# Rotation tables: one pass for all blocks, copies within DRAM, and plain loads of a block's tables

## The chip, the cores and the metric

The kernel runs on one core of one Trainium2 chip. The metric is the device time of one execution in microseconds. The core has five instruction queues that run side by side: TensorE (PE, matmuls), VectorE (DVE), ScalarE (ACT), GpSimd (POOL) and SyncE (SP), which in this kernel issues every transfer. Each of them works strictly in the order in which its instructions stand.

## What is computed

Two layers of a streaming encoder over 2048 frames of width 1024. Each layer projects its input, runs four groups of attention heads, gates them, projects their concatenation and normalises. Two of the groups rotate queries and keys by the frame's position; the change is about the tables of that rotation.

```python
def _rope(x, positions):
    d = x.shape[-1]
    inv_freq = ROPE_THETA ** (-jnp.arange(0, d, 2, dtype=jnp.float32) / d)
    ang = positions.astype(jnp.float32)[..., None] * inv_freq
    cos = jnp.cos(ang)[:, :, None, :]
    sin = jnp.sin(ang)[:, :, None, :]
    x1, x2 = jnp.split(x.astype(jnp.float32), 2, axis=-1)
    out = jnp.concatenate([x1 * cos - x2 * sin, x2 * cos + x1 * sin], axis=-1)
...
def _layer(x, mem, positions, w_in, ...):
    proj = x @ w_in
    ...
    ya = _banded_chunk_attention(aq, ak, av, A_PREV_CHUNKS, rel_bias=rel_bias)
    yb = _mla(bcq, bckv, bkr, positions, mla_q_norm, w_uq, mla_kv_norm, w_ukv)   # rotates 32 columns
    qc = _rope(cq, positions); kc = _rope(ck, positions)                         # 64 columns
    yc = _banded_chunk_attention(qc, kc, cv, SWA_PREV_CHUNKS, sinks=swa_sinks)
    ym = _memory_attention(mq, mem, w_mem_kv)
    gated = jnp.concatenate([ya * silu(ag), yb * silu(bg), yc * silu(cg), ym * silu(mg)], axis=-1)
    return _layer_norm(alpha * x + gated @ w_out, ln_gain, ln_bias)
```

## The kernel before

The frames are cut into four blocks of 512 (`BT`). A layer's first phase walks over the blocks; for each there are six units: `unit_c` (sliding window), `unit_m` (memory tokens) and `unit_a` (chunked attention), each for two pairs of heads, 0 and 1. A unit has a list of steps (`fill`: projections and what is made of them) and a list of score banks. `drive` runs the banks in order and mixes the next unit's steps among them. Then come `unit_b` (latent attention) over the blocks, and a third phase with the output projection and the norm. All products are done in two parts, a rounded high part and the rest (`whi`, `wlo`, `xh`, `xl`, `ph`, `pl`), whose splits are ACT's, DVE's and POOL's main work. What is written there is not yet the order on the engines: a scheduler in the compiler sorts the instructions of the whole program again, engine by engine, and each engine then keeps to that order.

A table has 128 rows (partitions) and 512 columns (frames). Its rows repeat: group 0 (`unit_c`, 64 columns to rotate) has 32 frequencies, four times over, group 1 (latents and `unit_b`) 16, eight times over. The sine's rows carry a sign that alternates by halves, from columns 2 and 3 of the constants `rc`. `trig(b, gs)` makes the cosine and sine of block `b` for the groups `gs`: it loads the positions to all rows, multiplies by the frequency, reduces the angle to the sine's range by a chain of DVE operations, takes two sines on ACT, and stores both tables to DRAM. It is called for block 0 and group 0 at the start, in `mem_kv`, among loads of the memory tokens (`xt<-in_mem`) and of x (`xt<-in_xT`); for block 0 and group 1 at the head of the first `unit_m`; and for block b + 1, both groups, as one step of `unit_a(l, b, 1)`. Where tables are used, two loads fetch them into the two tiles `cts`: `cts[0]` the cosine, `cts[1]` the sine. This is done 40 times in the program, in both layers. The rope of `unit_c` multiplies by both, moves the rows of the sine's product by four transfers (`us<-u`) and adds.

Steps draw temporary tiles from a ring called `tmp`, which `pi`, `ang`, `kk`, `xt` and many others share: a tile takes a buffer that earlier ones have left. PE waits for the splits and for the transfers of row maxima (`Y<-mr`) and copies (`Y<-Y`).

Of the kernel before, what the change touches and what calls it, by code (L numbers as in the profile page):

```python
# [11 lines left out]
F32 = mybir.dt.float32  # L12
# [4 lines left out]
OP = mybir.AluOpType  # L17
# [132 lines left out]
def hybrid(ctx, tc, x, mem, positions, w_in, rel_bias, q_norm, w_uq, kv_norm, w_ukv,  # L150
# [55 lines left out]
    def tmp(name, dt=F32):  # L206
        return sb.tile([128, BT], dt, name=name, tag="tmp", bufs=5)

    def rowcast(src, off, n):
        return bass.AP(tensor=src.tensor, offset=src.offset + off, ap=[[0, 128], [1, n]])  # L210
# [56 lines left out]

    cosT, sinT, memkv = {}, {}, {}
    h_src = [x[0, t * 128:(t + 1) * 128, :] for t in range(S // 128)]
# [8 lines left out]

    def trig(b, gs=(0, 1)):
        pi = tmp("pi", I32)  # L280
        dma(pi, rowcast(positions, b * BT, BT))
        pf = tmp("pf")
        nc.vector.tensor_copy(pf, pi)
        for g in gs:
            ang, kk = tmp("ang"), tmp("kk")
            nc.vector.tensor_scalar(ang, pf, rc[:, g:g + 1], None, op0=OP.mult)
            nc.vector.tensor_scalar(kk, ang, float(np.float32(1.0 / TWO_PI)), ROUND, op0=OP.mult, op1=OP.add)
            nc.vector.tensor_scalar(kk, kk, -ROUND, None, op0=OP.add)
            for pc in (PC1, PC2, PC3):
                stt(ang, kk, -pc, ang, op0=OP.mult, op1=OP.add)  # L290
            nc.vector.tensor_scalar(ang, ang, 3.1415925, -3.1415925, op0=OP.min, op1=OP.max)
            nc.vector.tensor_scalar(kk, ang, -1.0, None, op0=OP.mult)
            tt(kk, kk, ang, op=OP.max)
            nc.vector.tensor_scalar(kk, kk, -1.0, float(np.float32(math.pi / 2)), op0=OP.mult, op1=OP.add)
            act(ang, ang, AF.Sin)
            act(kk, kk, AF.Sin)
            nc.vector.tensor_scalar(ang, ang, rc[:, 2 + g:3 + g], None, op0=OP.mult)
            cosT[g, b] = dram.tile([128, BT], F32, name=f"cos{g}{b}")
            sinT[g, b] = dram.tile([128, BT], F32, name=f"sin{g}{b}")
            dma(cosT[g, b], kk)  # L300
            dma(sinT[g, b], ang)

# [429 lines left out]
    def unit_c(l, b, p, D):  # L732
# [4 lines left out]
        def tabl():  # L737
            dma(cts[0], cosT[0, b])
            dma(cts[1], sinT[0, b])
            if p == 0 and b:  # L740
                for k in range(2):
                    dma(f32(Kc[k][0])[:, 0:128], f32(Kc[k][0])[:, BT:BT + 128])
                    dma(f32(Kc[k][1])[0:64, 0:128], f32(Kc[k][1])[0:64, BT:BT + 128])
                dma(f32(Vc)[:, 0], f32(Vc)[:, 4])
# [81 lines left out]
    def latent(l, b, k, p, D):  # L826
# [6 lines left out]
        if k == 0:  # L833
            dma(cts[0], cosT[1, b])
            dma(cts[1], sinT[1, b])
            D["sums", b] = sb.tile([128, 3, 4], F32, name="sums", bufs=2)
# [119 lines left out]
    def unit_b(l, b, p, D):  # L956
# [13 lines left out]
        def loads():  # L970
            for k in (0, 2):
                dma(f32(lat[k]), f32(D["lathl"][k, b]).rearrange("p (s c) -> p s c", s=2))
            for z in range(2):
                dma(f32(lat[1])[64 * z:64 * z + 64, 0], f32(D["lathl"][1, b])[:, BT * z:BT * z + BT])
            dma(cts[0], cosT[1, b])
            dma(cts[1], sinT[1, b])
            for i in range(2):
# [231 lines left out]
    def mem_kv(kq):  # L1209
# [4 lines left out]
        dma(rc, rope_c)  # L1214
        trig(0, (0,))
        wload(1)
# [217 lines left out]
    for l in range(L):  # L1434
# [13 lines left out]
        else:  # L1448
            kq()
            load_mem(l)  # L1450
        units = []
        for b in range(NB):
            us = [unit_c(l, b, 0, D), None, None, None, None, None]
# [12 lines left out]
            if l == 0 and b == 0:  # L1466
                us[1][0].insert(0, (0.0, lambda: trig(0, (1,))))
            if l == 0 and b + 1 < NB:
                us[5][0].insert(2, (0.0, lambda b=b: trig(b + 1)))
            units += us  # L1470
# [64 lines left out]
```

## Time and profile before

| | |
|---|---|
| three runs, us | 2652.08, 2657.08, 2656.91; median 2656.91 |
| the profiled execution, us | 2656.69; its span 2654.9 |
| busy share of the span | PE 95%, DVE 70%, ACT 47%, POOL 40% |
| mean granted clock of PE | 0.981 |

The span runs from the first to the last instruction of the profiled execution. Busy is the time in which an engine had an instruction in work; for PE it is modelled, since matmuls overlap. The granted clock is the share of PE's full speed that the chip allowed.

### The profile page before, as it was taken

To read this page: it belongs to the slowest core of one execution; us is meant where nothing else is said; L and a number is where in the kernel's file an instruction comes from. 1 tells how busy PE (TensorE), PEld (TensorE's weight loads), DVE (VectorE), ACT (ScalarE), POOL (GpSimd) and SP (SyncE) were. 2 spreads that over 40 slices of the span, in tenths; PEclk is the share of its full clock that TensorE was granted. 3 is DMA by queue.
4 is the path that set the end of the run, shared out by engine and by line. 5 is a ranking of instruction groups with operands and counts; after the bars stand their busy time and mean duration, and the time that the engine had idled before them with its cause. 6 is when DMAs were issued, how large, how long until landed. Compare 5 with 4: busy or idle time off the path is not lost.

```text
span 2654.9 us, 36284 instructions
## 1 busy us (share of the span) xinstructions
PE 2518.4 (95%) x12312; PEld 2079.1 (78%) x12312; DVE 1871.5 (70%) x3309; ACT 1258.6 (47%) x2251; POOL 1070.8 (40%) x835
## 2 busy tenths in 40 slices
PE   7899999999999899989999999999999999998998
PEld 6777877877888788768877778788788777876786
DVE  5667768658666876878776566567577578588786
ACT  4545455545544566660025444454544455666200
POOL 4243334343344343354343434434433433435343
PEclk9999999999999999999999999999999999999999
DMA  6555345345335523254445443443443453233432
GB/s 213 162 158 164 109 137 159 113 128 165 107 125 158 158 77 92 76 160 140 146 138 154 156 144 121 134 139 118 137 136 115 145 166 108 62 116 96 151 122 85
DMA packets 176442, 350.90 MB, mean 132 GB/s; under 512 B 25688, under 2 KB 48944, under 8 KB 176256
## 3 DMA queue, kind: packets, MB, share of 16 engines
q1 hardware_dynamic: 176256, 348.58, 41.9%
q8 instruction: 98, 1.61, 0.3%
q14 instruction: 88, 0.72, 0.1%
HBM read 247.43 MB, written 68.02 MB: 119 GB/s over the span
## 4 chain that ended last, share of the span: by engine, by line
PE 60%; DVE 12%; issue 9%; DMA 5%; POOL 5%; ACT 3%; SPq 1%; POOLq 0%; DVEq 0%; ACTq 0%
PE pp L350 29%; PE sc L350 10%; PE pv L350 10%; PE mx L350 4%; PE po L350 3%; POOL xr L182 2%; PE up L350 2%; DVE pl L174 2%; DVE mcol L186 1%; DVE Y L174 1%; PE pst L856 1%; DVE gd L190 1%; DVE xl L174 1%; DVE e L190 1%; PE pvt L445 1%
## 5 line engine op out<-in xcount | busy, mean ns | idle before, releaser
L182 POOL TENSOR_TENSOR wlo<-raw,whi 128x1024 fp32r<-128x1024 f32 (+1 forms) x192 | 460.0, 2396 | 658.9 <-ACT whi L170 602.0
L350 PE MATMUL pp<-xh,whi 128*128 128x512 f32 x1472 | 590.7, 401 | 8.8 <-DVE Y L174 6.7
L350 PE MATMUL pp<-xl,whi 128*128 128x512 f32 x1472 | 582.5, 396 | 5.1 <-DVE xl L174 5.1
L350 PE MATMUL pp<-xh,wlo 128*128 128x512 f32 x1472 | 579.6, 394 | 0.0
L350 PE MATMUL sc<-Y 96*128 96x512 f32 (+16 forms) x1840 | 462.4, 354 | 14.6 <-DMA Y<-mr 8.7
L170 ACT ACTIVATE ph<-sc 128x512 fp32r<-128x512 f32 (+1 forms) x504 | 291.9, 579 | 321.8 <-PE sc L350 313.8
L174 DVE TENSOR_TENSOR pl<-p,ph 128x512 fp32r<-128x512 f32 (+2 forms) x361 | 300.9, 835 | 166.7 <-ACT p L170 157.2
L350 PEld LDWEIGHTS sc<-Y 96*128 96x128 f32 (+6 forms) x1840 | 319.7, 195 | 60.1 <-issue 9.5
L350 PE MATMUL pv<-ph,Y 128*128 128x512 f32 (+3 forms) x1396 | 357.3, 338 | 6.6 <-DVE e L178 5.3
L170 ACT ACTIVATE whi<-raw 128x1024 fp32r<-128x1024 f32 x192 | 203.5, 1060 | 326.9 <-PE pp L350 120.1
L350 PEld LDWEIGHTS pp<-xh,whi 128*128 128x128 f32 x1472 | 279.2, 190 | 64.8 <-issue 7.8
L350 PEld LDWEIGHTS pp<-xh,wlo 128*128 128x128 f32 x1472 | 278.3, 189 | 58.9
L350 PEld LDWEIGHTS pp<-xl,whi 128*128 128x128 f32 x1472 | 279.4, 190 | 49.7 <-DVE xl L174 6.6
L170 ACT ACTIVATE p<-sc 128x512 f32<-128x512 f32 (+1 forms) x504 | 291.1, 578 | 4.4 <-DVE pl L174 3.5
L182 POOL TENSOR_TENSOR pl<-p,ph 128x512 fp32r<-128x512 f32 (+1 forms) x143 | 186.9, 1307 | 263.0 <-ACT p L170 221.6
L350 PEld LDWEIGHTS pv<-ph,Y 128*128 128x128 f32 x1396 | 248.6, 191 | 42.5 <-issue 6.4
L350 PE MATMUL mx<-Y 128*128 128x256 f32 (+6 forms) x800 | 248.5, 338 | 21.1 <-DVE Y L178 10.6
L350 PE MATMUL pv<-pl,Y 128*128 128x512 f32 (+3 forms) x698 | 239.5, 343 | 22.8 <-DVE pl L174 14.9
L495 DVE CUSTOM_DVE_ANT_0 mx<-mx,bts 128x128 f32<-128x128 f32 (+3 forms) x352 | 171.8, 495 | 74.5 <-PE mx L350 67.4
L350 PEld LDWEIGHTS mx<-Y 128*128 128x128 f32 (+1 forms) x800 | 148.7, 191 | 75.2 <-DVE Y L178 17.4
L182 POOL TENSOR_TENSOR g<-g,e 128x128 f32<-128x128 f32 x192 | 117.1, 618 | 205.9 <-DVE e L190 198.6
L350 PE MATMUL po<-Y 128*128 128x512 f32 x768 | 177.3, 390 | 1.7 <-DVE xl L174 1.7
(241 smaller groups left out, 3763.8 us busy)
## 6 DMA issues: line engine op xcount, KB each, us to landing
raw<-in_w_in_dram SPq DMA_DIRECT2D x184, 512.0 KB
Y<-Y SPq DMA_DIRECT2D x144, 128.0 KB
gr<-gT SPq DMA_DIRECT2D x64, 256.0 KB
gT<-g SPq DMA_DIRECT2D x48, 256.0 KB
cts<-sin SPq DMA_DIRECT2D x40, 256.0 KB
cts<-cos SPq DMA_DIRECT2D x40, 256.0 KB
xt<-in_xT_dram SPq DMA_DIRECT2D x32, 256.0 KB
raw<-in_w_out_dram SPq DMA_DIRECT2D x16, 512.0 KB
```

The source lines that it names most:

```text
L170: return nc.scalar.activation(out, a, fn, **kw)
L174: return nc.vector.tensor_tensor(out, a, b, **kw)
L182: return nc.gpsimd.tensor_tensor(out, a, b, **kw)
L186: return nc.vector.reduce_max(out, a, axis=AX.X)
L190: return nc.vector.reciprocal(out, a)
L350: mm(o, lhs, rhs, start=start, stop=stop)
L445: nc.tensor.transpose(pt[:, j * 128:(j + 1) * 128], vf[:, j * 128:(j + 1) * 128], ident)
L495: nc.vector.tensor_tensor_reduce(m, m, table, op0=OP.add, op1=OP.max, scale=1.0, scalar=floor, accum_out=acc)
L856: mm(ps[:, 2 * t:2 * t + 2], sf[:, 128 * t:128 * t + 128], ones_f, start=True, stop=True)
```

## The change

The positions are loaded so that rows 32b to 32b + 31 hold those of block b (`trig_pos`, four transfers of 32 rows). One pass of the chain so makes the 32 rows of all four blocks at once (for group 1, 16 frequencies, twice over). `trig(g, pi)` is the list of the chain's 13 steps; it now ends with a negated sine, made by one more DVE operation, instead of a multiplication by the signs. Cosine, sine and negated sine are stored one below the other in one DRAM tile of 384 rows. `spread(g, b)` copies block b's rows out of it into two full tables of 128 rows, from DRAM to DRAM: the repeats are in the source's access pattern. `tload` loads these two tables, where the two loads of cosine and sine stood. The pass of group 0 and the copies for block 0 are called at the start, as `trig` was. The pass of group 1 is mixed, a step at a time, among the steps of the first `unit_m`. The copies of block b + 1 are single steps of `unit_c(l, b, 1)` for group 0 and of `unit_m(l, b, 1)` for group 1.

```diff
@@ -276,29 +276,65 @@
             act(rr[0:32, 0:c1 - c0], rf[0:32, 0:c1 - c0], AF.Copy)
             dma(f32(rowt)[:, c0:c1], f32(rr)[0:32, 0:c1 - c0])
 
-    def trig(b, gs=(0, 1)):
+    def trig_pos():
+
         pi = tmp("pi", I32)
-        dma(pi, rowcast(positions, b * BT, BT))
-        pf = tmp("pf")
-        nc.vector.tensor_copy(pf, pi)
-        for g in gs:
-            ang, kk = tmp("ang"), tmp("kk")
-            nc.vector.tensor_scalar(ang, pf, rc[:, g:g + 1], None, op0=OP.mult)
-            nc.vector.tensor_scalar(kk, ang, float(np.float32(1.0 / TWO_PI)), ROUND, op0=OP.mult, op1=OP.add)
-            nc.vector.tensor_scalar(kk, kk, -ROUND, None, op0=OP.add)
-            for pc in (PC1, PC2, PC3):
-                stt(ang, kk, -pc, ang, op0=OP.mult, op1=OP.add)
-            nc.vector.tensor_scalar(ang, ang, 3.1415925, -3.1415925, op0=OP.min, op1=OP.max)
-            nc.vector.tensor_scalar(kk, ang, -1.0, None, op0=OP.mult)
-            tt(kk, kk, ang, op=OP.max)
-            nc.vector.tensor_scalar(kk, kk, -1.0, float(np.float32(math.pi / 2)), op0=OP.mult, op1=OP.add)
-            act(ang, ang, AF.Sin)
-            act(kk, kk, AF.Sin)
-            nc.vector.tensor_scalar(ang, ang, rc[:, 2 + g:3 + g], None, op0=OP.mult)
-            cosT[g, b] = dram.tile([128, BT], F32, name=f"cos{g}{b}")
-            sinT[g, b] = dram.tile([128, BT], F32, name=f"sin{g}{b}")
-            dma(cosT[g, b], kk)
-            dma(sinT[g, b], ang)
+        for b in range(NB):
+            dma(pi[32 * b:32 * b + 32], bass.AP(tensor=positions.tensor, offset=positions.offset + b * BT,
+                                                ap=[[0, 32], [1, BT]]))
+        return pi
+
+    def trig(g, pi):
+
+        st = {}
+
+        def sc(o, i, *c, **k):
+            return lambda: nc.vector.tensor_scalar(st[o], st[i], *c, **k)
+
+        def red(pc):
+            return lambda: stt(st["a"], st["k"], -pc, st["a"], op0=OP.mult, op1=OP.add)
+
+        def start():
+            st["a"], st["k"] = tmp("ang"), tmp("kk")
+            nc.vector.tensor_copy(st["k"], pi)
+
+        def sine():
+            act(st["a"], st["a"], AF.Sin)
+            act(st["k"], st["k"], AF.Sin)
+            t = trigt[g] = dram.tile([3 * 128, BT], F32, name=f"trig{g}")
+            dma(t[0:128], st["k"])
+            dma(t[128 * (1 + g):128 * (2 + g)], st["a"])
+
+        def neg():
+            st["n"] = tmp("nsin")
+            nc.vector.tensor_scalar(st["n"], st["a"], -1.0, None, op0=OP.mult)
+            dma(trigt[g][128 * (2 - g):128 * (3 - g)], st["n"])
+        return [start,
+                sc("a", "k", rc[:, g:g + 1], None, op0=OP.mult),
+                sc("k", "a", float(np.float32(1.0 / TWO_PI)), ROUND, op0=OP.mult, op1=OP.add),
+                sc("k", "k", -ROUND, None, op0=OP.add)] + [red(pc) for pc in (PC1, PC2, PC3)] + [
+                sc("a", "a", 3.1415925, -3.1415925, op0=OP.min, op1=OP.max),
+                sc("k", "a", -1.0, None, op0=OP.mult),
+                lambda: tt(st["k"], st["k"], st["a"], op=OP.max),
+                sc("k", "k", -1.0, float(np.float32(math.pi / 2)), op0=OP.mult, op1=OP.add),
+                sine, neg]
+
+    def spread(g, b):
+
+        t = trigt[g][32 * b:32 * b + 1, 0:1]
+        n = 32 >> g
+        for k, (o, ap) in enumerate(((0, [[0, 4], [BT, 32], [1, BT]]),
+                                     (128 * BT, [[0, 2 + 2 * g], [(128 + g * n) * BT, 2], [BT, n], [1, BT]]))):
+            r = tabt[g, b, k] = dram.tile([128, BT], F32, name=f"tab{g}{b}{k}")
+            i = bass.AP(tensor=t.tensor, offset=t.offset + o, ap=ap)
+            if k:
+                dma(r.rearrange("(a s n) c -> a s n c", s=2, n=n), i)
+            else:
+                dma(r.rearrange("(a n) c -> a n c", n=32), i)
+
+    def tload(g, b):
+        for k in range(2):
+            dma(cts[k], tabt[g, b, k])
@@ -735,8 +771,7 @@
         fill = []
 
         def tabl():
-            dma(cts[0], cosT[0, b])
-            dma(cts[1], sinT[0, b])
+            tload(0, b)
             if p == 0 and b:
                 for k in range(2):
                     dma(f32(Kc[k][0])[:, 0:128], f32(Kc[k][0])[:, BT:BT + 128])
@@ -831,8 +866,7 @@
         if n == 64:
             nc.gpsimd.memset(sf[64:128], 0.0)
         if k == 0:
-            dma(cts[0], cosT[1, b])
-            dma(cts[1], sinT[1, b])
+            tload(1, b)
             D["sums", b] = sb.tile([128, 3, 4], F32, name="sums", bufs=2)
         later(0.8, lambda: dma(D["lat"][k, b][:n], cf[:n]))
         if k == 1:
@@ -972,8 +1006,7 @@
                 dma(f32(lat[k]), f32(D["lathl"][k, b]).rearrange("p (s c) -> p s c", s=2))
             for z in range(2):
                 dma(f32(lat[1])[64 * z:64 * z + 64, 0], f32(D["lathl"][1, b])[:, BT * z:BT * z + BT])
-            dma(cts[0], cosT[1, b])
-            dma(cts[1], sinT[1, b])
+            tload(1, b)
             for i in range(2):
                 kh, kl = kpart(i, b)
                 dma(f32(kh)[96:101], f32(rowt)[26:31, 0:BT])
@@ -1212,7 +1245,9 @@
         wload(0)
         f()
         dma(rc, rope_c)
-        trig(0, (0,))
+        for f_ in trig(0, trig_pos()):
+            f_()
+        spread(0, 0)
         wload(1)
         run_fill(st)
         wsplit(0)
@@ -1464,9 +1500,11 @@
             if b == 0:
                 us[2] = ([(0.0, lambda: (ka(), bias_tables(l, D)))] + us[2][0], us[2][1])
             if l == 0 and b == 0:
-                us[1][0].insert(0, (0.0, lambda: trig(0, (1,))))
+                us[1] = (mix(us[1][0], [(0.0, lambda: tg.extend(trig(1, trig_pos())))]
+                             + [(0.0, lambda: tg.pop(0)())] * 13 + [(0.0, lambda: spread(1, 0))]),) + us[1][1:]
             if l == 0 and b + 1 < NB:
-                us[5][0].insert(2, (0.0, lambda b=b: trig(b + 1)))
+                for g in range(2):
+                    us[3 + g][0].insert(2, (0.0, lambda b=b, g=g: spread(g, b + 1)))
             units += us
         for p in range(2):
             for b in range(NB):
```

Three places on the engines show what this moves; buffer numbers are the program's own. The first is DVE in block 2, around its last units, where the tables of block 3 were made. Before, these twelve rows ended it (`ang` and `kk` belong to the tables; `g` and `e` are the gate's numerator and denominator, `pl` a rest, `Y` queries and keys):

```order
L174 TENSOR_TENSOR kk<-kk,ang 128x512
L291 TENSOR_SCALAR ang<-ang 128x512
L294 TENSOR_SCALAR kk<-kk 128x512
L292 TENSOR_SCALAR kk<-ang 128x512
L174 TENSOR_TENSOR Y<-pp,Y 64x512
L174 TENSOR_TENSOR kk<-kk,ang 128x512
L297 TENSOR_SCALAR ang<-ang,rc 128x512
L294 TENSOR_SCALAR kk<-kk 128x512
L297 TENSOR_SCALAR ang<-ang,rc 128x512
L174 TENSOR_TENSOR g<-pv,g 64x512
L178 SCALAR_TENSOR_TENSOR e<-e,pv 64x512
L174 TENSOR_TENSOR Y<-pp,Y 64x512
```

Now, from the rest `pl` ahead of the same gate on:

```order
L174 TENSOR_TENSOR pl<-p,ph 128x512
L174 TENSOR_TENSOR Y<-ef,Y 1x512
L190 RECIPROCAL e<-e 128x128 x2
L174 TENSOR_TENSOR pl<-p,ph 128x512
L174 TENSOR_TENSOR Y<-pp,Y 64x512 x2
L174 TENSOR_TENSOR g<-pv,g 64x512
L178 SCALAR_TENSOR_TENSOR e<-e,pv 64x512
L178 SCALAR_TENSOR_TENSOR Y<-pp,Y 64x512 x2
```

The table rows between the splits and the gate are gone; fourteen further rows of the same call stood ahead of those shown, among other work.

The second place is SP at the start. Before, where `xt<-in_mem` are pieces of the memory tokens, `xt<-in_xT` of x, and `cos` the first table's store:

```order
L325 DMA raw0_85<-in_w_mem_kv_dram 128x1024
L410 DMA xt_212<-in_mem_dram 128x256
L410 DMA xt_216<-in_mem_dram 128x256
L410 DMA xt_220<-in_mem_dram 128x256
L325 DMA raw1_86<-in_w_mem_kv_dram 128x1024
L410 DMA xt_224<-in_mem_dram 128x256
L410 DMA xt_307<-in_xT_dram 128x512
L274 DMA rf_261<-in_rows_dram 32x512
L274 DMA rf_266<-in_rows_dram 32x128
L410 DMA xt_329<-in_xT_dram 128x512
L410 DMA xt_349<-in_xT_dram 128x512
L300 DMA cos00_207<-kk_193 128x512
```

Now (`trig0` is the tile of 384 rows, `nsin` the negated sine, `tab000` the first full table of group 0 and block 0):

```order
L306 DMA trig0_208<-ang_193 128x512
L446 DMA xt_219<-in_mem_dram 128x256
L305 DMA trig0_208<-kk_194 128x512
L446 DMA xt_223<-in_mem_dram 128x256
L311 DMA trig0_208<-nsin_211 128x512
L1462 DMA gn_77<-in_mla_kv_norm_dram 128x1
L446 DMA xt_227<-in_mem_dram 128x256
L446 DMA xt_231<-in_mem_dram 128x256
L333 DMA tab000_214<-trig0_208 4x16384
```

The last four pieces of the memory tokens stood ahead of the cosine's store and now stand behind the first store of the tables, between the three stores. On PE the matmuls that use these pieces stand nearly where they stood.

The third place is SP in block 1, around the rope of `unit_c` for the second pair of heads. Before:

```order
L480 DMA gT0_4_1_111<-g_2585 128x512
L621 DMA bts1_93<-dbt03_1080 128x640
L488 DMA Y_91<-mr_3120 1x4x128
L723 DMA us_3131<-u_3130 32x512 x4
L325 DMA raw1_86<-in_w_in_dram 128x1024
L834 DMA cts0_87<-cos11_1957 128x512
L835 DMA cts1_88<-sin11_1958 128x512
```

Now:

```order
L333 DMA tab020_3065<-trig0_208 4x16384
L759 DMA us_3115<-u_3114 32x512 x4
L361 DMA raw0_85<-in_w_in_dram 128x1024
L361 DMA raw1_86<-in_w_in_dram 128x1024
L524 DMA Y_91<-mr_3104 1x4x128
L337 DMA cts0_87<-tab110_1733 128x512
L337 DMA cts1_88<-tab111_1735 128x512
```

The shift `us<-u` has a copy within DRAM straight ahead of it: its destination is shown as four rows of 16384 elements (the second table of group 1 has eight of 8192). The loads of `cts` name other tensors and stand where they stood.

## Rows read from the trace of the kernel before

**Rows 1.** The page: busy time by engine; the queue of all data transfers.
```profile
PE 2518.4 (95%) x12312; PEld 2079.1 (78%) x12312; DVE 1871.5 (70%) x3309; ACT 1258.6 (47%) x2251; POOL 1070.8 (40%) x835
...
q1 hardware_dynamic: 176256, 348.58, 41.9%
```

**Rows 2.** Stretches: length; busy (instructions) of PE, PEld, DVE, ACT, POOL; PEclk, DMA, GB/s.
```profile
0.00:700.00 700.00, 646.38 (x3220) 536.85 (x3221) 478.26 (x870) 351.64 (x596) 274.63 (x205) 0.97 0.48 149
198.00:240.00 42.00, 36.62 (x166) 29.61 (x165) 31.98 (x57) 20.30 (x30) 15.59 (x12) 0.92 0.49 159
240.00:383.00 143.00, 140.40 (x714) 117.00 (x713) 96.82 (x176) 72.43 (x127) 55.41 (x38) 0.99 0.41 126
383.00:440.00 57.00, 49.70 (x239) 41.32 (x238) 43.43 (x79) 26.08 (x42) 21.46 (x14) 0.94 0.50 153
440.00:590.00 150.00, 147.56 (x761) 122.87 (x760) 99.99 (x190) 77.87 (x135) 62.15 (x43) 1.00 0.41 126
590.00:650.00 60.00, 52.89 (x251) 44.07 (x250) 45.65 (x81) 27.96 (x44) 19.69 (x13) 0.91 0.46 149
```

**Rows 3.** PE in order of time; in brackets its idle time and what ended it.
```profile
213.93 1.19 PE L350 MATMUL pv<-ph,Y 128*128 128x512 f32 x2 [5.34 <-DVE e L178]
...
387.27 0.50 PE L350 MATMUL mx<-Y 128*128 128x256 f32 x2 [2.07 <-DVE Y L178]
...
395.70 0.50 PE L350 MATMUL mx<-Y 128*128 128x256 f32 x2 [1.76 <-DVE e L178]
...
416.11 0.76 PE L350 MATMUL pp<-xh,whi 128*128 128x512 f32 x1 [3.47 <-DVE Y L174]
...
598.37 0.80 PE L350 MATMUL mx<-Y 128*128 128x256 f32 x2 [3.87 <-DVE Y L178]
...
625.91 0.47 PE L350 MATMUL pp<-xh,whi 128*128 128x512 f32 x1 [3.22 <-DVE Y L174]
```

**Rows 4.** DVE, then ACT, in order of time, from 592 us.
```profile
594.98 2.61 DVE L283 CAST pf<-pi 128x512 f32<-128x512 int32 x1 [3.32 <-DMA pi<-in_positions_dram]
...
615.96 1.28 ACT L170 ACT_TABLE_LOAD   x1
620.27 0.64 ACT L170 ACTIVATE ang<-ang 128x512 f32<-128x512 f32 x1 [3.02 <-DVE kk L174]
```

**Rows 5.** A stretch behind the first of these waits, columns as in rows 2.
```profile
215.00:218.00 3.00, 3.00 (x9) 2.35 (x8) 2.94 (x3) 2.94 (x5) 1.84 (x1) 0.56 0.38 141
```

**Rows 6.** Waits of PE, DVE, ACT, 60 to 700 us: total, times, longest.
```profile
PE ptab L1188 <- DMA tr<-ext: 4.4, 1, 4.4
...
DVE t L174 <- DMA us<-u: 7.5, 4, 2.2
...
ACT xh L170 <- DMA xt<-in_xT_dram: 6.5, 7, 2.1
```

**Rows 7.** The tile `ang`: nanoseconds of one, least, median, most.
```profile
L178 DVE SCALAR_TENSOR_TENSOR ang<-kk,ang x24: 676/680/2889, 16.2 to 619.0; 128x512 f32<-128x512 f32 x24
...
L291 DVE TENSOR_SCALAR ang<-ang x8: 411/416/428, 19.3 to 620.2; 128x512 f32<-128x512 f32 x8
...
L170 ACT ACTIVATE ang<-ang x8: 630/630/636, 22.5 to 622.5; 128x512 f32<-128x512 f32 x8
```

**Rows 8.** The start: SP, ACT, SP, ACT, PE, PE in order of time.
```profile
18.44 0.33 SPq L410 DMA_DIRECT2D xt<-in_mem_dram  x1
...
20.47 0.42 ACT L170 ACTIVATE Y<-xt 128x256 fp32r<-128x256 f32 x1 [1.73 <-DMA xt<-in_mem_dram]
...
23.64 0.33 SPq L300 DMA_DIRECT2D cos<-kk  x1
...
24.04 1.04 ACT L170 ACTIVATE whi<-raw 128x1024 fp32r<-128x1024 f32 x1
...
25.14 0.50 PE L350 MATMUL pp<-Y,whi 128*128 128x256 f32 x2 [1.69 <-ACT whi L170]
...
35.58 0.44 PE L445 MATMUL pvt<-identr,vf 128*128 128x128 f32 x2 [2.24 <-ACT vf L170]
```

More of the change, by code (lines that the diff above doesn't have):

```diff
@@ L266, in mla_kv @@
         return [4096 + 1024 * (b - 1), 4096 + 3072 + 1024 * (b - 1), 4096 + 6144 + 1536 * (b - 1)]
-    cosT, sinT, memkv = {}, {}, {}
+    trigt, tabt, memkv = {}, {}, {}
     h_src = [x[0, t * 128:(t + 1) * 128, :] for t in range(S // 128)]
@@ L1451, in hybrid @@
         units = []
+        tg = []
         for b in range(NB):
```

## The prediction

> **What bounds the kernel now.** I read the page first, then stretches of the span, then the waits inside the stretches that stand out. TensorE (PE) is busy for 95% of the span and VectorE (DVE) for 70% [rows 1], and nearly the same matmuls run whatever the tables do, so a change can only win or lose what PE idles, and what it runs at the lower clock. The table of stretches [rows 2] shows where that is. Two quiet stretches, 240 to 383 us and 440 to 590 us, have PE idle for 2.6 of 143 us and 2.4 of 150 us: 1.7%. Three short ones between them, at 198, 383 and 590 us, have it idle for 5.4, 7.3 and 7.1 us, and in these DVE is the engine that is full: 32.0 of 42, 43.4 of 57, 45.7 of 60 us. Each of the three holds one call of `trig(b + 1)`. PE's own rows [rows 3] name what it waited for: six waits of 5.3, 2.1, 1.8, 3.5, 3.9 and 3.2 us, 19.8 in all, and each ended with a DVE instruction that has nothing to do with tables (`e`, `Y`). DVE's and ACT's rows around the last of them [rows 4] show why: DVE first stands 3.3 us for the positions and then takes 2.6 us for the cast; further on, in the order shown above, it works through the chains of both groups back to back, and ACT, which has already loaded the table for the sine, waits 3.0 us for an argument while the exponentials queue behind it.
>
> [...]
>
> The order of PE, DVE, ACT and POOL differs between the two programs only up to block 3 of the first layer's first phase; PE's matmuls are the same, one by one, from the 3184th of some 12,200 on, and by 700 us PE had started some 3220 [rows 2]. So I look for the whole effect ahead of about 700 us and expect the remaining 1950 us to stay.
>
> **Term A, the three lumps.** The change makes eight passes of the chain into two: six group passes go, and three casts with their position loads. A pass is three `ang<-kk,ang` at 0.68 us and one maximum, which I count at the same, and seven operations like the clamp at 0.42 [rows 7]: 2.7 + 2.9, some 5.7 us of DVE. The ACT part is two sines at 0.63 [rows 7], and a table load of 1.28 us ahead of each lump [rows 4], with another behind it, since the exponentials follow. The new negated sine adds one operation of some 0.42 us to each of the two passes left. DVE so loses some 6 x 5.7 = 34 us, but only what PE waited for counts: 19.8 us of named waits plus six times 1.3 us of low clock is 27.6. The three stretches are 159 us long, and at the quiet stretches' 1.7% an idle of 2.7 us would remain: 25 us. I take 24. Bounds: 28 above, if nothing remains; 12 below, if half of these waits only pass on to the next producer (a rival, below).
>
> **Term B, block 0.** The second group's pass was one lump near 90 us and becomes 13 steps mixed among a unit's other steps. PE waited there 4.4 us for a bias table [rows 6], whose chain stood behind the lump on DVE. In the new order the first of these table matmuls is PE's matmul 520 instead of 449, so the chain has the time of 71 more matmuls; but its first load now stands behind a table copy on SP. Between 0 and 6 us of gain, I take 3.
>
> **Term C, the start.** This one costs. Before, the last piece of `mem` was issued at 18.4 us, and ACT took it at 20.5, 2.0 us after its issue; the cosine's store came later, at 23.6, and PE had its next weights at 25.1 [rows 8]. In the new order the last four such loads stand behind the stores of the tables on the one queue, SP, and the last two wait for buffers that these stores must first empty. With the same chain and a few more `xh`/`xl` steps inside it, I put the cosine's store at 25 us; it must land, then the last piece of `mem` must (2.0 us each, going by the 2.0 above): 29. ACT's and DVE's split of it (0.42 us on ACT [rows 8], as much on DVE), its matmuls and the split of the next weight (1.04 us on ACT [rows 8]) bring PE's next weights to about 31.5 instead of 25.1: a loss of 6.4. Against it, the splits of x that ACT and DVE did after 25 us are now done earlier, and a wait of 2.2 us of PE for ACT, which ended at 35.6 [rows 8], may shrink. I take 6; bounds 2 and 9.
>
> **Term D, the copies from DRAM to DRAM.** They are new, and the trace has none. Sixteen go out, two at the start and fourteen in blocks 0 to 2, 256 KB written by each. All transfers together moved 348.58 MB in 41.9% of 16 engines' span [rows 1]: 19.6 GB/s for one engine while it works. Spread over all sixteen, a copy takes 0.84 us; on one engine, 13.4. The order shows the destination as four rows of 64 KB, or eight of 32 KB for group 1's second table, where a plain load has 128 rows. If one row goes to one engine, a copy holds four engines for 3.3 us, or eight for 1.7; the fourteen then hold them for 10 x 3.3 + 4 x 1.7 = 40 us (from 12 to 188 with the two ends). I take that, since the row is the only piece in sight. [...]
>
> What queues behind a copy: everything that SP issues next, because it is the only queue for data. Weights come early; and in the list of PE's waits between 60 and 700 us a transfer stands just once, with the 4.4 us of term B [rows 6], so most transfers have slack. Not so the rope's shift `us<-u`: DVE stood for it 4 times, 7.5 us in all, and ACT 6.5 us for pieces of x [rows 6]. Four of the fourteen copies stand within a few rows ahead of such a shift. If each is late by 3.3 us, DVE stands 13 us. At 595 us DVE lost 3.3 us waiting and about 2.2 us by the slow cast (2.61 where its plain operations on such a tile take 0.42 [rows 7]), 5.5 in all, and PE waited 3.9 [rows 3, 4]: some two thirds. Two thirds of 13 us is 9. I take 9 for all copies; bounds 0 and two thirds of 40, that is 27. The loads of the finished tables replace loads of the same size, and eight position loads of 64 KB replace five of 256 KB: nothing, since both were issued far ahead of their use; without that cover each table load would add some 3 us at a rope.
>
> **Sum.** -24 - 3 + 6 + 9 = -12 us. The profiled execution took 2656.69 us (span 2654.9), the median of the three runs is 2656.91, so they can be used alike: 2657 - 12 = 2645.
>
> **Rivals.**
> - *The copies hold the queue (slower).* The place is SP behind the fourteen copies; the price is the upper bound of D. For it: shifts and pieces of x already have engines standing for them [rows 6], and each engine works in order. Against it: PE's waits for transfers are few. It gives -24 - 3 + 6 + 27 = +6, 2663 us. It decides from 21 us of loss on PE, 1.5 us for each copy. [...]
> - *The waits pass on (no change).* DVE is free, but PE stands at the same places for ACT, for an `mx` in its order or for a transfer, so A is 12: -12 - 3 + 6 + 9 = 0, 2657. For it: ACT's exponentials and DVE's own queue are close behind everywhere. Against it: the quiet stretches, which have the same work without the lumps, idle 1.7%.
> - *The change doesn't do what it says.* Excluded for the lumps: in the new order the three are gone from DVE. Possible for block 0, which is term B's lower end.
>
> **Chances.** Forecast 0.62, waits pass on 0.20, copies hold the queue 0.18. One measurement here resolves about 0.2%, 5.3 us. The forecast's own range is 2630 to 2651, from A and C at their better bounds to D at twice its value. To leave out no more than 2 in 10, the range goes up past the middle of the slower rival: 2629 to 2666. Faster than 2651.6: 0.62; between: 0.20; above 2662.2: 0.18.
>
> **What would show it.** A: in the new profile the stretches that held the lumps have PE idle for under 3% and no wait of over 2 us on `e` or `Y`; DVE's busy time is some 35 us less, ACT's some 15. C: PE takes its third memory weight after 30 us. B: no 4 us wait for `tr<-ext`. D: waits of DVE for `us<-u` and of ACT for `xt` stay near 7 us each in the first 700; if they triple, the slower rival is right. From 700 us on the two traces run in step. Wrong it would be if the start costs over 15 us (the weights' loads behind the first two copies are the place to look), or if copies take far longer than 3.3 us.

## The result: 71 us slower

| | before | after |
|---|---|---|
| four runs each, us | 2652.08 to 2657.08, median 2655.14 | 2723.37 to 2729.09, median 2726.14 |
| ratio | | 1.0266, 95% interval 1.025 to 1.0281 |
| span of the profiled execution, us | 2654.9 | 2724.0 |

The page of the changed kernel, the lines that answer to [rows 1]:

```profile
PE 2539.2 (93%) x12312; PEld 2088.1 (77%) x12312; DVE 1839.0 (68%) x3240; ACT 1242.9 (46%) x2233; POOL 1068.9 (39%) x835
...
q1 hardware_dynamic: 174616, 349.36, 41.0%
```

DVE has lost 32.5 us of work and ACT 15.7, as forecast (some 35 and 15); ACT's table loads, 1.28 us each, are 5 instead of 11. PE runs the same 12,312 matmuls, but is busy 20.8 us longer, at a granted clock of 0.976 over the span instead of 0.981. The stretches say where, answering to [rows 2]; the two that end at 210 and 770 us are cut at the same matmuls in every kernel below, after some 812 and after 2400 more:

```profile
0.00:700.00 700.00, 603.16 (x2893) 494.25 (x2894) 394.83 (x702) 299.45 (x517) 241.20 (x187) 0.94 0.43 134
0.00:210.00 210.00, 164.40 (x811) 135.74 (x812) 106.03 (x206) 91.64 (x160) 69.20 (x67) 0.95 0.51 159
210.00:770.00 560.00, 504.74 (x2405) 412.86 (x2405) 337.27 (x594) 243.30 (x418) 200.87 (x138) 0.94 0.41 127
```

The kernel before, cut at the same matmuls:

```profile
0.00:187.00 187.00, 161.73 (x813) 134.31 (x814) 111.49 (x208) 94.31 (x164) 74.35 (x70) 0.96 0.57 177
187.00:698.00 511.00, 482.65 (x2400) 400.89 (x2399) 365.96 (x662) 256.23 (x430) 199.42 (x136) 0.97 0.44 138
```

I call them the start (812 matmuls) and the middle (2400). The start takes 210 us instead of 187, the middle 560 instead of 511, together 72 us: the whole difference. The remaining 9,100 matmuls take as long as before, within 3 us, as forecast. The middle, which was to gain 24 us, lost 49: PE idles 55.3 us there instead of 28.4, and is busy 22 us longer for the same matmuls, at a granted clock of 0.94 instead of 0.97. Nothing is full: DVE works 337 of 560 us, transfers take 41%.

The lumps are gone: of the chain, which [rows 7] had 24 times up to 619 us, six rows are left, the last at 110 us.

```profile
L178 DVE SCALAR_TENSOR_TENSOR ang<-kk,ang x6: 674/691/694, 19.0 to 110.0; 128x512 f32<-128x512 f32 x6
```

The start, in SP's, ACT's and PE's order of time, answering to [rows 8]:

```profile
26.16 0.40 SPq L305 DMA_DIRECT2D trig<-kk  x1
...
28.65 0.80 SPq L446 DMA_DIRECT2D xt<-in_mem_dram  x2
29.51 0.67 SPq L333 DMA_DIRECT2D tab<-trig  x1
...
31.68 0.75 ACT L170 ACTIVATE Y<-xt 128x256 fp32r<-128x256 f32 x2 [1.50 <-DMA xt<-in_mem_dram]
34.34 1.06 ACT L170 ACTIVATE whi<-raw 128x1024 fp32r<-128x1024 f32 x1 [1.91 <-PE pp L386]
...
28.43 1.04 PE L386 MATMUL pp<-Y,whi 128*128 128x256 f32 x3 [14.07 <-ACT Y L170]
...
35.45 0.67 PE L386 MATMUL pp<-Y,whi 128*128 128x256 f32 x2 [0.34 <-ACT whi L170]
```

PE stands 14.1 us for a piece of the memory tokens (before, but for the very first, 2.2 at most), and has its third memory weight at 35.5 us; I had put it at 31.5. The waits that [rows 6] showed, for the same stretch of 60 to 700 us:

```profile
PE ptab L1221 <- DMA tr<-ext: 3.0, 1, 3.0
...
DVE t L174 <- DMA us<-u: 2.2, 1, 2.2
...
ACT xh L170 <- DMA xt<-in_xT_dram: 7.5, 2, 6.3
```

So transfers are hardly waited for more than before: in the middle PE waits for none in either kernel, DVE 3.3 us instead of 11.5, ACT 14.9 instead of 17.7. What PE waits for in the middle is many things, mostly for 1 to 3 us each: for DVE 34 us in all, for ACT 11, for POOL 6. The place with the most is 260 to 280 us, where PE is busy for 12.9 us, at a granted clock of 0.78:

```profile
260.00:280.00 20.00, 12.90 (x56) 10.36 (x55) 14.31 (x17) 7.48 (x14) 7.65 (x6) 0.78 0.32 102
```

PE's waits there in order of time, then what DVE does, then POOL:

```profile
268.44 0.73 PE L386 MATMUL pv<-ph,Y 128*128 128x512 f32 x2 [1.21 <-ACT ph L170]
271.73 0.79 PE L386 MATMUL pv<-pl,Y 128*128 128x512 f32 x1 [2.55 <-DVE pl L174]
...
277.24 0.69 PE L386 MATMUL pv<-pl,Y 128*128 128x384 f32 x1 [3.33 <-DVE pl L174]
...
279.00 0.63 PE L386 MATMUL pp<-xh,whi 128*128 128x512 f32 x1
```

```profile
266.88 3.39 DVE L190 RECIPROCAL e<-e 128x128 f32<-128x128 f32 x4
270.19 0.63 DVE L174 TENSOR_TENSOR xl<-xt,xh 128x512 fp32r<-128x512 f32 x1
270.73 0.94 DVE L174 TENSOR_TENSOR pl<-p,ph 128x512 fp32r<-128x512 f32 x1
271.60 2.84 DVE L174 TENSOR_TENSOR xl<-xt,xh 128x512 fp32r<-128x512 f32 x1
274.36 3.15 DVE L174 TENSOR_TENSOR pl<-p,ph 128x512 fp32r<-128x512 f32 x2
...
271.08 5.55 POOL L182 TENSOR_TENSOR wlo<-raw,whi 128x1024 fp32r<-128x1024 f32 x2
```

DVE does four reciprocals of a gate and two splits of x ahead of the `pl` that PE stands for, and PE has nothing else in its order meanwhile: counted in the trace these are about matmuls 1040 to 1138, 36 of attention in a row and only then 63 of projections (`pp`). DVE is also slow here: the second `xl` takes 2.84 us and the first `pl` of the last row 2.82, where the `xl` ahead took 0.63, and POOL is at two weight splits for most of that time. Between its matmuls 320 and 3223 the new order has five runs of more than 24 matmuls without a projection, up to 69 long; the order of before has none. No table is made here, and the nearest copies are issued at 245.0 and 282.8 us. That gave the theory that I then tested: **the loss is the order that the compiler gave all engines once the copies were in the program**, against **the copies themselves hold transfers** (my slower rival), and against **the one pass of the chain and its start**.

### The profile page after: what moved, and what is told of

The parts are those of the page before. It is cut to its first block, busy times and chain, and to the rows that moved or that the text cites. A ratio compares the mean times of both kernels' runs of the same rounds, so it can differ in the third digit from the quotient of the medians.

```text
span 2724.0 us, 36124 instructions
## 1 busy us (share of the span) xinstructions
PE 2539.2 (93%) x12312; PEld 2088.1 (77%) x12312; DVE 1839.0 (68%) x3240; ACT 1242.9 (46%) x2233; POOL 1068.9 (39%) x835
## 4 chain that ended last, share of the span: by engine, by line
PE 59%; DVE 11%; issue 10%; POOL 5%; DMA 5%; ACT 3%; SPq 1%; POOLq 0%; DVEq 0%; ACTq 0%
PE pp L386 29%; PE pv L386 10%; PE sc L386 10%; PE mx L386 4%; PE po L386 3%; POOL xr L182 2%; PE up L386 2%; DVE pl L174 2%; DVE mcol L186 1%; POOL wlo L182 1%; DVE Y L174 1%; DVE e L190 1%; PE pst L890 1%; ACT Y L170 1%; DVE mx L531 1%
## 5 line engine op out<-in xcount | busy, mean ns | idle before, releaser
L386 PEld LDWEIGHTS pp<-xh,wlo 128*128 128x128 f32 x1472 | 280.0, 190 | 68.8 <-POOL wlo L182 10.1
L386 PEld LDWEIGHTS pv<-pl,Y 128*128 128x128 f32 x698 | 134.4, 193 | 58.2 <-DVE pl L174 32.3
```

Of the source, the lines that this page charges most:

```text
L386: mm(o, lhs, rhs, start=start, stop=stop)
```

## The experiments

Times of a single run are given with their difference to the kernel before on the same chip; chips differ by some 0.5% (before: 2641 to 2656). On one chip eleven runs of the kernel before lay between 2644.68 and 2655.80 us, so differences of single runs of under some 10 us are not clear of noise.

**Wide or narrow copies, and either one's order.** The first run changes the order of each copy's loops, so that the slowest has 32 or 16 steps instead of 4 or 2; number and bytes of the copies stay. It leaves out the alternating signs of the second table, and so do the runs below with wide copies, but for e7 and e12:

```diff
-            if k:
-                dma(r.rearrange("(a s n) c -> a s n c", s=2, n=n), i)
-            else:
-                dma(r.rearrange("(a n) c -> a n c", n=32), i)
+            m = n if k else 32
+            i = bass.AP(tensor=t.tensor, offset=t.offset + o, ap=[[BT, m], [0, 128 // m], [1, BT]])
+            dma(r.rearrange("(a n) c -> n a c", n=m), i)
```

> Each copy's slowest dimension is now 32 or 16 rows (each row copied to its repeats in turn) instead of 4 repeats or pairs; same number of copies, same bytes. The second table loses its alternating signs here. The compiler's order moves back close to that of before (PE: 323 of the first 4000 rows differ from before, against 881 in the changed kernel). Theory Q (the narrow copies hold the transfers behind them): about 2650, since a copy then occupies sixteen engines for about a microsecond. Theory O (the order that the compiler gave the first phase around the narrow copies costs the 70 us): about 2650 too. Theory S (the one pass itself, its steps and the start cost it): stays at 2715 to 2726.

The microsecond on sixteen engines is term D's 0.84 us, an estimate from [rows 1]; how many engines a wide copy takes no view shows.

The compiler then chooses another order. The next two runs exchange the orders: a table `ORDERED` holds, for each engine, the sequence that the other program has, and neighbours are tied without adding a wait.

```diff
+    for seq in ORDERED:
+        prev = None
+        for n in seq:
+            i = nm.get(f"I-{n}")
...
+            if prev is not None:
+                tc.add_manual_dep(i, prev, mybir.DependencyInfo(mybir.DependencyClass.NoSync, mybir.DependencyReason.DATA),
+                                  reason="order")
+            prev = i.name
```

> The wide copies of the run above, but every engine is held to the order of the changed kernel (an order table adds edges between neighbours on each engine; nothing else differs). Theory Q: 2650 or a little above, since no copy is narrow any more. Theory O: stays at 2715 to 2726, since the order is that of the changed kernel. A split between the two gives the share of each.

> The changed kernel's own narrow copies, with correct tables, but every engine held to the order that the compiler chose for the wide copies. Theory Q: 2700 to 2726, since the narrow copies are all there. Theory O: 2640 to 2660, a little above the run with wide copies by what the copies themselves cost.

| | order of the changed kernel | order chosen with wide copies |
|---|---|---|
| narrow copies | the changed kernel, +71 | e3: 2655.6, +7.0 |
| wide copies | e2: 2715.35, +66.8 | e1: 2647.37, -1.2 |

In the traces the exchanged orders are the same, instruction for instruction, on all five engines. The order costs 64 to 68 us, with either copies. The narrow copies cost 4 to 8 more than the wide ones, with either order, which is within the noise of single runs. The one pass and its place at the start are in e1 too, which takes as long as before, so they are not the loss. The start and the middle of the run with narrow copies in the other order, then of the one with wide copies in the changed kernel's order:

```profile
0.00:212.00 212.00, 165.23 (x813) 135.72 (x814) 112.26 (x209) 94.75 (x164) 75.44 (x70) 0.98 0.54 171
212.00:702.00 490.00, 475.91 (x2400) 394.10 (x2399) 322.24 (x591) 240.98 (x412) 199.94 (x135) 0.99 0.44 140
```

```profile
0.00:208.00 208.00, 162.79 (x811) 134.53 (x812) 106.15 (x206) 91.65 (x160) 69.50 (x67) 0.96 0.51 160
208.00:764.00 556.00, 505.00 (x2402) 413.99 (x2401) 336.99 (x593) 242.56 (x417) 201.57 (x138) 0.94 0.41 128
```

The middle goes with the order: 490 us against 556. Of the 70 us between 560 and 490, 41 are idle time of PE (55.3 against 14.1) and 29 are busy time of the same matmuls at the lower granted clock, 0.94 against 0.99 (504.7 us busy against 475.9). Of the idle time, 34 us end with a DVE instruction in the one and 10 in the other.

**No copies, and copies alone.** The calls of `spread` are left out; the tables so lack their repeats and the blocks' own rows:

```diff
-        spread(0, 0)
...
-            dma(cts[k], tabt[g, b, k])
+            dma(cts[k], trigt[g][128 * k:128 * k + 128])
```

> The changed kernel without any copy: a table load reads 128 plain rows of the stored tile, so the repeats and the blocks' own rows are left out; the order is the compiler's own and close to that of before. Against the run with narrow copies in the wide copies' order (2656) it prices the sixteen narrow copies themselves: by my term for them 9 us, so 2647; by the slower rival 27 us, so 2629. Against the wide copies (2647) it prices those: 0 to 4.

2639.03, 2.4 us faster than before. Sixteen narrow copies so cost 7.0 + 2.4 = 9.4 us, the wide ones 1.2, from single runs on two chips. The start and the middle of this run are 13 and 5 us shorter than those with narrow copies (212 and 490):

```profile
0.00:199.00 199.00, 161.30 (x815) 135.18 (x816) 111.39 (x207) 95.47 (x164) 72.80 (x69) 0.91 0.56 171
199.00:684.00 485.00, 473.54 (x2400) 390.85 (x2399) 323.19 (x594) 241.50 (x413) 202.80 (x136) 1.00 0.43 137
```

The opposite, the kernel of before with a `spread` that copies rows of x for nobody:

```diff
+        spread(0, 0)
...
+                for g in range(2):
+                    us[3 + g][0].insert(2, (0.0, lambda b=b, g=g: spread(g, b + 1)))
```

> The kernel of before, its tables made as before, plus sixteen narrow copies of the same two shapes at the places of the change; they read x and nobody reads them. Theory O (the order around the copies): the compiler moves 857 of PE's first 4000 rows for them, with a stretch of 48 attention matmuls and one of 63 projection matmuls in a row, so 2700 to 2725. Theory Q (only the transfers themselves): 2660 to 2667. If the loss needs the one-pass chain, about 2657.

2736.93, 95.5 us slower, more than the whole change and more than I had expected. In its trace, too, the start and the middle are longer (202 and 577 us), and five runs of more than 24 matmuls have no projection. The loss needs no other part of the change: narrow copies in the program are enough to get such an order. Why the compiler chooses it stays open.

**The start.** Wide copies with their signs (each second table in two copies), and the first pass called behind the memory tokens' splits:

```diff
-        for f_ in trig(0, trig_pos()):
-            f_()
-        spread(0, 0)
         wload(1)
         run_fill(st)
...
         wload(3)
+        for f_ in trig(0, trig_pos()):
+            f_()
+        spread(0, 0)
         early()
```

> Wide copies with correct signs (the second table in two copies), and the first pass of the chain with its stores and copies called behind the splits of the memory tokens instead of ahead of them. If the table work ahead of the memory tokens is what the start loses (matmul 312 begins at 94 us with wide copies, at 76 before), some 15 to 18 us come back: 2630. If the start loses elsewhere, 2647 as with wide copies.

2625.51, 16.0 us faster than before, and 14.8 better than wide copies with the early pass (-1.2). Its start and middle:

```profile
0.00:190.00 190.00, 158.00 (x813) 130.49 (x813) 113.42 (x207) 92.36 (x161) 76.28 (x69) 0.95 0.58 184
190.00:677.00 487.00, 474.27 (x2403) 391.42 (x2403) 325.15 (x594) 243.74 (x417) 201.74 (x137) 1.00 0.45 143
```

Timed again, in six runs against eleven of the kernel before, it is 0.8% faster, clear of noise:

> The kernel with wide copies and the first pass behind the memory tokens again, timed in rounds against the kernel before: a ratio of 0.994, 16 us faster, as in its single look.

2627.75 against 2647.47, ratio 0.9918 (0.9903 to 0.9933).

**Tables without copies.** Once by loads that read the stored rows with their repeats (e4), once by storing each row four times from on-chip memory, behind the memory tokens (e8):

```diff
+                dma(cts[0], bass.AP(tensor=t.tensor, offset=t.offset, ap=[[0, 4], [BT, 32], [1, BT]]))
...
```

> No copies at all: each table load reads the stored rows from DRAM with the repeats in its own access pattern, the cosine in one transfer, the sine and its negative in two or four of 64 or 32 rows (74 more transfers on SP in all). Theories Q and O: about 2645, as forecast for the change without its term for the copies (2657 - 24 - 3 + 6 = 2636) plus some issue time on SP. Theory S: 2715 to 2726.

```diff
+            v = trigt[g, k].rearrange("(b a n) c -> a b n c", a=4, n=32)
+            dma(v[a], src)
...
```

> No copies within DRAM: the finished rows are stored four times from on-chip memory straight into full tables (eight stores a group), the loads are plain, and the first pass stands behind the memory tokens as in the run above. Same order of the first phase as before within 235 of PE's 4000 rows. If the destination's four outer rows do not confine a store, 2625 to 2632; if they do, sixteen narrow stores cost some 8 more, 2633 to 2640.

Both missed: 2698.41 (+49.8) and 2644.88 (+3.4). The first phase of e4 is fast (its first 3211 matmuls take 691 us, 698 before), and PE's order from there on is nearly that of before (57 of 9089 matmuls stand elsewhere); what it loses comes behind, where 129 of the 168 narrow loads lie that took the place of 80 plain ones. The rest of e4, then the same matmuls of the run with wide copies (e1):

```profile
691.00:2690.00 1999.00, 1886.98 (x9103) 1554.45 (x9101) 1389.09 (x2440) 908.94 (x1657) 790.65 (x630) 0.98 0.39 123
```

```profile
697.00:2640.00 1943.00, 1871.36 (x9102) 1541.97 (x9100) 1390.92 (x2441) 907.72 (x1657) 797.55 (x630) 0.99 0.40 127
```

And PE's waits in 700 to 2640 us, e4, then e1:

```profile
PE sc L381 <- DMA Y<-mr: 20.7, 8, 4.8
PE mx L381 <- DMA Y<-xh: 11.9, 7, 3.4
```

```profile
PE sc L384 <- DMA Y<-mr: 8.2, 5, 3.5
```

This fits the slower rival's mechanism, narrow transfers ahead of short ones that PE needs: PE stands 20.7 us for `Y<-mr` instead of 8.2, and 11.9 us for `Y<-xh`, where e1 has 1.5 us at most. The stretch is 56 us longer (1999 - 1943), for 129 of them 0.4 us each; 24 us of it are the waits shown, the rest I did not follow.

**Which engine's order.** Wide copies, with only some engines held to the changed kernel's order; the compiler orders the others around them.

> Wide copies (no alternating signs, as before in these); only TensorE is held to the order of the changed kernel, the other four engines are ordered by the compiler around it. If the loss comes from TensorE's own sequence (attention matmuls in runs of up to 61 without a projection between them, projections in runs of up to 63): all of the some 66 us over the kernel before, as with all engines held. If it comes from where the transfers stand on SP: about the time of before. A part of it: the others' order, ACT's and DVE's, holds the rest.

> Wide copies; only SP is held to the order of the changed kernel, copies at its late places included; TensorE keeps a sequence with one run of 49 attention matmuls and one of 28. If the transfers' order holds the loss: 50 to 66 us over before. If TensorE's sequence does: 10 to 25 us over, for the two runs that are left.

> Wide copies; only VectorE is held to the order of the changed kernel. TensorE's order alone cost 22 us over before and SP's alone 12, all five together 67. If the rest sits in where the splits, reciprocals and adds stand on VectorE: 30 us or more over before. If it only comes from several engines being out of step with each other: 0 to 15.

> Wide copies; only ScalarE is held to the order of the changed kernel. As in the run with VectorE's order: 30 us or more over before if the rest sits in ScalarE's places, 0 to 15 if it does not.

> Wide copies; ScalarE, VectorE and GpSimd together are held to the order of the changed kernel, TensorE and SP are ordered around them by the compiler. If these three hold the rest: 40 to 60 us over before, and nearly all 67 if TensorE's own sequence only follows from theirs. If nothing but the combination with TensorE's sequence costs: under 25.

> Wide copies; TensorE and SP together are held to the order of the changed kernel, the other three are ordered around them. If the shares of the engines add: 22 + 12 = 34 us over before. If these two are the whole of it and the others only follow: 60 or more.

| held to the changed kernel's order | us | against before |
|---|---|---|
| TensorE (e9) | 2669.61 | +22.1 |
| SP (e10) | 2659.90 | +12.4 |
| ScalarE (e14) | 2676.26 | +26.1 |
| VectorE (e13) | 2703.45 | +53.3 |
| TensorE and SP (e16) | 2674.55 | +24.4 |
| ScalarE, VectorE, GpSimd (e15) | 2719.61 | +69.5 |
| all (e2) | 2715.35 | +66.8 |

Holding the three engines that split, scale and add is enough for all of it, and VectorE alone for most. The shares don't add, since the others are ordered around the one that is held. The other way round, the changed kernel with one engine in the good order:

> The changed kernel with its narrow copies; only TensorE is held to the order that the compiler gave it with wide copies, everything else is ordered by the compiler, and the copies stand spread to the end of block 2 again. If TensorE's sequence holds the loss: 7 to 15 us over before, as with all engines held to that order. If SP's, DVE's and ACT's places do: 40 us or more over.

> The changed kernel with its narrow copies; only VectorE is held to the order that the compiler gave it with wide copies. If VectorE's order holds the loss: 10 to 25 us over before (7 with all engines held to that order, 39 with TensorE alone). If it does not: 40 us or more over.

2686.41 (+38.9) and 2717.03 (+64.1): neither of the two engines tried mends it alone, and the expectation that VectorE's good order might did not come true. The compiler again orders the rest around the narrow copies; in the second run some 830 of PE's first 4000 matmuls stand elsewhere than in the good order. Last, one guess at what it is in VectorE's order, the rows of four reciprocals seen at 267 us:

> Wide copies and VectorE's order of that kernel with one difference: the four reciprocals of a gate stand in one row of four, at the place of the last, for all seventeen gates of the first phase's first 800 rows (the kernel with wide copies has three such rows of four and 38 single ones, the changed kernel seven and 14). If the clumps of reciprocals are what VectorE's order costs: 25 to 50 us over before. If they are only a part of it, as one place in the trace, where TensorE stood 7.1 us behind such a clump, would have it: 5 to 20. If none: 0.

2652.45, 0.5 us faster than before: such rows alone cost nothing that one run can show. Which rows of VectorE's order it is stays open. The slow operations seen at 271 us are a candidate that no run here tests: in the middle 14 of DVE's operations take over 1 us longer than their shape does elsewhere in the changed kernel's order (with either copies), 5 to 8 in the good orders (e1, e3, e5, e7), all beside one of POOL's; but the kernel before has 13.

## Why the prediction was wrong

- **The step that failed** is the sum: it prices the lumps, the start and the copies, and has no term for the order. I had seen that the order of four engines differs up to matmul 3184 and used it only to say where to look; I took the new order to be as good as the old one but for the work removed. It cost 70 us in the middle (560 instead of 490 us with the same copies and the same instructions). That it is the order is shown by the two exchanges; that narrow copies bring it about, by e6 and e1; what in the order costs the time is shown only as far as VectorE.
- **Term A (-24)** holds where the order is good: with narrow copies the middle takes 490 us instead of 511, with wide ones 487 (e7): -21 to -24. The first of these is 14 us of idle time (14.1 instead of 28.4) and 7 of busy time, at a granted clock of 0.99 instead of 0.97. The 1.3 us of low clock that A counts six times are an estimate from one stretch, 3 us at 0.56 [rows 5], so 3 x (1 - 0.56); no run shows them for each of the six waits, and the 7 us of busy time stand in their place.
- **Term D (+9)** came near by luck. e3 against e5, whose orders are nearly the same, gives 9.4 us for sixteen narrow copies, with the noise of single runs on two chips. But D was the rope's shift, late behind the fourteen copies, and in e3 DVE stands for `us<-u` 7.2 us from 60 to 700 us, as before (7.5). By the stretches the two copies of the start weigh more (13 us) than the fourteen (5). In the changed kernel's trace the semaphore of a copy with four steps has five events and that of a copy with two has three, one more than the steps; a wide copy (e1) has sixteen, as a plain load of a table has. The last event comes 5.4 us after the issue for the first tables, 6.0 for group 1's second and 8.0 for group 0's second, 3.7 for a wide copy and 3.3 for a plain load (medians). D's engines, four for 3.3 us or eight for 1.7, were an estimate; group 1's second table has five events where D counted eight engines, and how many engines work at one copy no view shows.
- **Terms B and C (+3 together)** were mis-sized: the start lost 23 us. The mechanism of C was the one I gave, stores of tables ahead of the last pieces; the third weight came at 35.5, 10.3 us late instead of 6.4, since ACT had the last pieces at 31.7 instead of 29 and then stood 1.9 us for `pp` on PE, which I had not counted. B gave 1.4 of 3 (the wait for `tr<-ext` is 3.0 instead of 4.4). I followed the chain only as far as that weight: PE idles 20 us more in the whole start (45.6 instead of 25.3), 12 of them in waits for ACT's `Y` (20.3 instead of 8.4). Of the 23 us, 20 go when the pass is moved and the copies are wide (e7's start is 190).
- **The rivals.** The slower one had the right side and the wrong mechanism: waits for `us<-u` did not triple but fell to 2.2 us (7.2 in e3), those for pieces of x stayed near 7 (7.5, 10.1 in e3). It fits e4, where 129 narrow loads stand ahead of what PE waits for and the stretch is 56 us longer, and is small with sixteen copies (9.4 us). The waits did not pass on either: with the good order the middle gains what A said.

With the good order and all else as it is, e3, the change comes out at +7 in one run, instead of -12: its middle gains 21 us, its start loses 25 (212 instead of 187).

## What to carry to other kernels

Where a compiler sorts the instructions, a change has a part that no row of the old profile prices: the new order. Count how much of it moves, build the change's parts one by one and see which of them moves it, and doubt a forecast for work that is merely reordered; holding the order fixed while the transfers change, and the other way round, separates the two. Here the copies with the most steps outermost brought the better order (-1.2 against +71) and cost 8 us less than the narrow ones with that order held, which one run each can't tell from noise; the pass of the chain behind the memory tokens, for a piece of which PE had stood 14.1 us, was worth 14.8 us more (e7 against e1).

## What the runs showed of the hardware

In e8 eight narrow stores held up the queue and the engines that waited for them: of 256 KB each and with four outer steps, they are issued from 35.8 us on, nearly one behind the other. Three stretches of e8:

```profile
0.00:40.00 40.00, 17.39 (x96) 15.77 (x96) 25.34 (x43) 18.84 (x31) 18.13 (x35) 0.89 0.69 209
40.00:50.00 10.00, 0.00 (x0) 0.00 (x0) 0.00 (x0) 0.00 (x0) 0.00 (x0) 0.50 0.27 103
50.00:60.00 10.00, 5.02 (x23) 4.62 (x23) 0.85 (x2) 1.72 (x5) 0.00 (x0) 0.50 0.51 145
```

And SP there in order of time (start, length; x is how many), where one issue took 0.33 us shortly ahead of it, then ACT and PE:

```profile
34.06 0.33 SPq L356 DMA_DIRECT2D raw<-in_w_mem_kv_dram  x1
34.44 0.47 SPq L274 DMA_DIRECT2D rf<-in_rows_dram  x1
35.81 3.01 SPq L303 DMA_DIRECT2D trig<-kk  x4
38.86 3.08 SPq L274 DMA_DIRECT2D rf<-in_rows_dram  x1
41.98 2.40 SPq L303 DMA_DIRECT2D trig<-ang  x2
44.48 3.44 SPq L303 DMA_DIRECT2D trig<-nsin  x2
47.97 4.14 SPq L467 DMA_DIRECT2D Y<-Y  x1
...
53.35 8.69 SPq L1270 DMA_DIRECT2D mk<-Y  x3
...
50.06 0.38 ACT L170 ACTIVATE vf<-pp 128x256 f32<-128x256 f32 x1 [10.25 <-DMA trig<-kk]
...
50.49 0.69 PE L476 MATMUL pvt<-identr,vf 128*128 128x128 f32 x2 [23.73 <-ACT vf L170]
```

From 40 to 50 us no engine works at all, while the transfer engines are busy for 27%, some four of 16. ACT stands 10.25 us for the stores of `kk`: by its semaphore's events the fourth of them, issued by 38.8 us, lands at 50.0, and PE stands for ACT. What is issued behind them is late too: a load of `rf` issued ahead of them, at 34.4 us, lands after 4.7 us, a smaller one behind them, at 38.9, after 11.3; on SP itself the first issue takes 0.47 us, the second 3.08, and that of `Y<-Y` at 48.0 us 4.14. Against e7, where PE stands 15.5 us for `vf`, this costs 8 us; a wait of 10.3 us for `tr<-ext`, which e7 does not have, is most of the rest of the 19 us between the two. Whether eight wide stores would do the same no run shows. PE's granted clock is 0.50 from 40 to 60 us, also when work comes back, and 0.89 over the 40 us ahead.
